# Transposes of the first half of the merged matrix write to PSUM banks of the attention's pool

## The chip, the cores and the metric

The kernel runs on one core of a Trainium2 chip. The metric is the time of one execution on the device in microseconds (us). Several runs of the kernel were timed, and one execution was profiled on the hardware.

## The reference

Two layers of a gated trunk over 256 rows of width 1024, with three branches per layer (an attention in blocks, an attention on selected keys, an attention on a memory), and a final norm. All is fp32. What matters here is the end of each layer: every branch's output (256 x 512) is multiplied by its matrix of w_branch, gated, and the three are summed; the sum goes through w_out.

```python
    ys = jnp.stack([ya, yb, ym], axis=2)
    up = jnp.einsum('bsnw,nwd->bsnd', ys, w_branch)
    gates = jax.nn.sigmoid(mix.reshape(b, s, N_BRANCH, D_MODEL))
    merged = jnp.sum(gates * up, axis=2)
    return x + jnp.einsum('bsd,de->bse', merged, w_out)
```

## The kernel before

**Products.** An fp32 product is made of three fp32r products, `mm3` (lines 105 to 107): high part by high part, high by low and low by high. `split` makes the parts: ACT copies the high part (L101), DVE subtracts it (L102). Weights come in units of 128 x 1024 through `unit`: SP loads `raw` (four buffers), ACT casts it to `whi`, DVE subtracts to `wlo` (four buffers each). So a cast waits until PE has used the unit four before it, and a load until DVE has subtracted the unit four before it.

**PSUM.** There are three pools of banks: pmm with four (tiles mm), psa with two (tiles sc), pst with two (tiles pt). The pools psa and pst serve the attention, the small transposes and, at the layer's end, the accumulators of w_out. A pool gives its banks out in the order in which the program asks for them.

**The end of a layer.** The 256 rows are two tiles t of 128, the 1024 columns of the merged matrix two halves b of 512. `mixes(b, n)` makes the gate by a tanh on ACT (L538). `merge(b, n, ...)` multiplies branch n's output by its weights (24 matmuls, 512 wide), DVE multiplies by the gate (L551) and adds to the sum acc (L553). After the third branch of a half, `merged_T(b, acc)` transposes the sum, per row tile t four 128 x 128 transposes into one bank (L562, a group), ACT writes the high part mgh (L564) and DVE the low part mgl (L565); both are needed by w_out, whose eight units of weights k = 0 to 7 (half 0 for k below 4, half 1 above) accumulate in banks sc and pt per row tile. In layer 0 each row tile has two accumulators of 512; in layer 1 the second tile has 512, 256 and 256 (the last in a bank mm), and behind w_out follow the additions to x (L621), the squares for the norm (L622), the factor rs on POOL (L628), the multiplications by the gain and by rs (L624, L635, L637, L632) and the stores.

**Names used below.** B: the 24 matmuls of `merge(0, 2)`. C: the 24 of `merge(1, 2)`. Both read the branch output in the tile bq. T00, T01: the two groups of transposes of half 0, row tiles 0 and 1; T10, T11: those of half 1. O1 to O8: the eight units of w_out's weights.

**The order.** The program asks for C's banks behind those of `merged_T(0)`: the list `todo` ends with (0, 2) and (1, 2), and `merged_T(b, ...)` follows where n is 2. A scheduler makes each engine's queue from it; it may place later work earlier on an engine, but not past its pool's order of banks. Each engine then works through its queue in order. PE's queue decides how B, the groups, C and w_out follow on each other.

Of the kernel before, what the change touches and what calls it, by code (L numbers as in the profile page):

```python
# [34 lines left out]
def trunk(ctx, tc, x, x_t, mem, mem_t, consts, norm_g, gains, w_grp, w_idx, w_mix, w_kv, w_br, w_o, final_g, out):  # L35
# [6 lines left out]
    pmm = ctx.enter_context(tc.tile_pool(name="pmm", bufs=4, space=PSUM))  # L42
    psa = ctx.enter_context(tc.tile_pool(name="psa", bufs=2, space=PSUM))
    pst = ctx.enter_context(tc.tile_pool(name="pst", bufs=2, space=PSUM))

    def bank(pool, tag):
        return pool.tile([P, 512], F32, tag=tag, name=tag)
# [432 lines left out]
    for l in range(L):  # L480
# [74 lines left out]
        def merged_T(b, acc):  # L555

            bs = slice(4 * b, 4 * b + 4)
            for t in range(NT):
                tt = slice(t * P, (t + 1) * P)
                pt = bank(pmm, "mm")  # L560
                for i in range(4):
                    nc.tensor.transpose(pt[:, i * P:(i + 1) * P], acc[:, t, i * P:(i + 1) * P], ident)  # L562
                pt = pt.rearrange("p (a b) -> p a b", b=P)
                nc.scalar.activation(mh[:, bs, tt], pt, AF.Copy, scale=0.5)  # L564
                nc.vector.scalar_tensor_tensor(ml[:, bs, tt], pt, 0.5, mh[:, bs, tt].bitcast(F32),  # L565
                                               op0=ALU.mult, op1=ALU.subtract)
# [7 lines left out]
        for j, (b, n) in enumerate(todo):  # L574
            if j == 3 and l + 1 < L:
                mhl = mem_tiles()
                memT = big.tile([P, KC, S], F32, tag="big", name="memT")
                load_after(memT, mem_t)
                mem_prep(l + 1, memT, *mhl, range(KC))
            merge(b, n, mxs[j], mxs[2 * b])  # L580
            if j != 2 and len(mxs) < 6:
                mxs.append(mixes(*todo[len(mxs)]))
            if n == 2:
                merged_T(b, mxs[2 * b])
# [26 lines left out]
    for t in range(NT):  # L611
# [4 lines left out]
        for c in cuts[t]:  # L616
            a, b = c
# [90 lines left out]
```

## Time and profile before

| | us |
|---|---|
| median of 3 runs | 632.03 |
| lowest, highest | 631.92, 632.26 |
| the profiled execution, its time | 632.53 |
| the profiled execution, its span | 630.7 |

The span is from the first to the last instruction; the time holds 1.8 us more that lie around it. Sums below are made against the profiled execution, and then moved to the median, which is 0.5 us lower. A row of a timeline gives the start, the duration, the engine, the line of the kernel, the operation, the tile written and the tiles read; in square brackets stands how long the engine was idle before it and what released it. A matmul's duration holds its passage through the array, so successive ones overlap: what it takes of PE's time is the distance of the starts.

### The profile page before, as it was taken

What the parts mean: (1) busy time and instruction counts of PE and PEld (TensorE: products, weight loads), DVE (VectorE), ACT (ScalarE), POOL (GpSimd) and SP (SyncE); (2) the same over time, 40 slices, a digit from 0 to 9 for tenths busy, and PEclk for the clock granted to TensorE, in tenths of its full rate; (3) what the DMA queues carried; (4) which work ended last, traced back from release to release, by engine and by line L of the source; (5) the groups of instructions that cost most, each with busy time, mean ns of one, the idle gap of its engine ahead of it and who ended that gap; (6) DMA issues with size and microseconds to landing.
All of it is one profiled execution on the core that took longest, in us unless ns stands there. A gap on an engine that the chain in (4) does not pass through costs nothing.

```text
span 630.7 us, 10090 instructions
## 1 busy us (share of the span) xinstructions
PE 613.3 (97%) x3518; PEld 536.2 (85%) x3518; DVE 489.7 (78%) x1002; ACT 391.0 (62%) x721; POOL 90.4 (14%) x159
## 2 busy tenths in 40 slices
PE   7999999999999999998999999999999999999894
PEld 5989989888988888887889998998898888888783
DVE  5678889998867878786584778998887787778563
ACT  6758555686657856744464666657675696654342
POOL 1213004003200212110020100310321011221002
PEclk8999999999999999999999999999999999999998
DMA  8966554456554554574655755454555545465521
GB/s 290 347 202 224 173 164 144 134 169 200 160 171 145 180 179 138 197 235 125 194 171 137 265 165 164 140 160 149 181 177 165 165 136 176 160 197 180 155 68 67
DMA packets 31731, 109.57 MB, mean 174 GB/s; under 512 B 3648, under 2 KB 3648, under 8 KB 31552
## 3 DMA queue, kind: packets, MB, share of 16 engines
q1 hardware_dynamic: 31392, 108.39, 53.6%
q8 instruction: 28, 0.46, 0.3%
q10 hardware_dynamic: 288, 0.52, 0.2%
q14 instruction: 23, 0.19, 0.1%
HBM read 107.86 MB, written 1.05 MB: 173 GB/s over the span
## 4 chain that ended last, share of the span: by engine, by line
PE 94%; DVE 2%; ACT 1%; DMA 1%; POOL 1%; issue 1%; SPq 0%; POOLq 0%; DVEq 0%; ACTq 0%
PE mm L107 25%; PE mm L106 25%; PE mm L105 25%; PE sc L107 2%; PE sc L106 2%; PE sc L105 2%; PE sc L297 2%; PE pt L217 1%; PE pt L323 1%; PE pt L107 1%; PE sc L294 1%; PE pt L106 1%; PE pt L105 1%; DMA raw<-in_w_kv 1%; DVE wlo L102 1%
## 5 line engine op out<-in xcount | busy, mean ns | idle before, releaser
L102 DVE TENSOR_TENSOR wlo<-raw,whi 128x1024 fp32r<-128x1024 f32 (+2 forms) x201 | 241.6, 1207 | 73.1 <-ACT whi L101 70.2
L101 ACT CAST whi<-raw 128x1024 fp32r<-128x1024 f32 (+2 forms) x201 | 204.0, 1017 | 122.4 <-PE mm L107 57.6
L107 PE MATMUL mm<-whi,hl 128*128 128x512 f32 (+2 forms) x416 | 160.0, 386 | 1.4 <-DVE hl L102 1.4
L106 PE MATMUL mm<-wlo,hh 128*128 128x512 f32 (+2 forms) x416 | 160.5, 386 | 0.0
L105 PE MATMUL mm<-whi,hh 128*128 128x512 f32 (+2 forms) x416 | 160.1, 387 | 0.0
L107 PEld LDWEIGHTS mm<-whi,hl 128*128 128x128 f32 x416 | 78.1, 188 | 15.8 <-DVE hl L102 1.6
L106 PEld LDWEIGHTS mm<-wlo,hh 128*128 128x128 f32 x416 | 78.3, 188 | 13.8
L105 PEld LDWEIGHTS mm<-whi,hh 128*128 128x128 f32 x416 | 78.1, 188 | 13.3
L284 POOL TENSOR_SCALAR pr<-pr,rinv 128x256 f32<-128x256 f32 (+1 forms) x80 | 44.3, 571 | 221.1 <-DVE rinv L282 219.0
L107 PE MATMUL mm<-hh,wlo 128*128 128x256 f32 x256 | 73.3, 287 | 0.0
L106 PE MATMUL mm<-hl,whi 128*128 128x256 f32 x256 | 72.9, 285 | 0.0
L105 PE MATMUL mm<-hh,whi 128*128 128x256 f32 x256 | 72.4, 283 | 0.0
L106 PEld LDWEIGHTS mm<-hl,whi 128*128 128x128 f32 x256 | 49.0, 191 | 0.2
L105 PEld LDWEIGHTS mm<-hh,whi 128*128 128x128 f32 x256 | 49.0, 191 | 0.2
L107 PEld LDWEIGHTS mm<-hh,wlo 128*128 128x128 f32 x256 | 48.9, 191 | 0.0
L279 ACT ACTIVATE pr<-tm,nb 128x128 f32<-128x128 f32 (+1 forms) x80 | 36.7, 460 | 11.5 <-DVE nb L313 10.7
L206 POOL TENSOR_TENSOR qf<-rt,rt 128x128 f32<-128x128 f32 (+2 forms) x24 | 14.6, 619 | 129.0 <-DVE rt L205 129.0
L553 POOL TENSOR_TENSOR mx<-mx 128x512 f32<-128x512 f32 x8 | 12.4, 1551 | 51.3 <-DVE mx L551 51.3
L551 DVE SCALAR_TENSOR_TENSOR mx<-mx,mm 128x512 f32<-128x512 f32 x24 | 16.4, 684 | 3.5 <-PE mm L107 3.4
L538 ACT ACTIVATE mx<-mm 128x512 f32<-128x512 f32 x24 | 14.3, 596 | 7.7 <-PE mm L107 7.5
L105 PE MATMUL mm<-mh,whi 128*128 128x256 f32 x64 | 18.1, 284 | 0.0
L106 PE MATMUL mm<-ml,whi 128*128 128x256 f32 x64 | 18.1, 283 | 0.0
(259 smaller groups left out, 1140.9 us busy)
## 6 DMA issues: line engine op xcount, KB each, us to landing
raw<-in_w_grp SPq DMA_DIRECT2D x80, 512.0 KB, 4.7
raw<-in_w_mix SPq DMA_DIRECT2D x48, 512.0 KB, 4.0
raw<-in_w_br SPq DMA_DIRECT2D x24, 512.0 KB, 3.8
raw<-in_w_o SPq DMA_DIRECT2D x16, 512.0 KB, 4.5
raw<-in_w_kv SPq DMA_DIRECT2D x15, 512.0 KB, 6.0
raw<-in_w_idx SPq DMA_DIRECT2D x16, 292.0 KB, 3.0
memT<-in_mem_t SPq DMA_DIRECT2D x4, 256.0 KB, 5.8
xr<-in_x SPq DMA_DIRECT2D x2, 512.0 KB, 6.5
```

Source lines behind the costliest of these rows:

```text
L101: nc.scalar.copy(hi, src)
L102: nc.vector.tensor_sub(lo, src, hi.bitcast(F32))
L105: nc.tensor.matmul(o, lh, rh, start=start, stop=False, skip_group_check=True)
L106: nc.tensor.matmul(o, lh, rl, start=False, stop=False, skip_group_check=True)
L107: nc.tensor.matmul(o, ll, rh, start=False, stop=stop, skip_group_check=True)
L206: nc.gpsimd.tensor_tensor(dst[:, :, 0:16], t1[:, :nh], t2[:, :nh], op=ALU.add)
L279: nc.scalar.activation(pr[:, i, :nk], tm[:, i, :nk], AF.Exp, bias=nb[:, i:i + 1], scale=scale, accum_out=rsum[:, i:i + 1])
L284: nc.gpsimd.tensor_scalar(pr[:, i, :nk], pr[:, i, :nk], rinv[:, i:i + 1], 1.0, op0=ALU.mult, op1=ALU.mult)
L297: nc.tensor.matmul(scs[i][:, 1, :], qT[:, h, P:], k[:, b, :], start=b == 0, stop=b == 1, skip_group_check=True)
L538: lambda t, i, ps: nc.scalar.activation(mx[:, t], ps, AF.Tanh, scale=0.5))
L551: nc.vector.scalar_tensor_tensor(mx[:, t], mx[:, t], 1.0, ups[t], op0=ALU.add, op1=ALU.mult)
L553: (nc.gpsimd, nc.vector)[n - 1].tensor_tensor(acc[:, t], acc[:, t], mx[:, t], op=ALU.add)
```

## The change

One line in `merged_T`: for half b = 0 the bank of a group of transposes comes from the pool pst (tile pt); for half 1 it comes from pmm (tile mm) as before.

```diff
             for t in range(NT):
                 tt = slice(t * P, (t + 1) * P)
-                pt = bank(pmm, "mm")
+                pt = bank(*((pst, "pt"), (pmm, "mm"))[b])
                 for i in range(4):
                     nc.tensor.transpose(pt[:, i * P:(i + 1) * P], acc[:, t, i * P:(i + 1) * P], ident)
```

The queues change with it. First PE in layer 0, before, where B ends (mm_3252 is B's second row tile, mm_3293 T00, sc_3363 and pt_3364 w_out's accumulators of row tile 0, whi_3368 O1):

```order
L107 MATMUL mm_3252<-whi_3260,bq_1987 128x512
L562 MATMUL mm_3293<-cst_82,mx_2604 128x128 x4
L105 MATMUL sc_3363<-whi_3368,mgh_2602 128x512
L106 MATMUL sc_3363<-wlo_3369,mgh_2602 128x512
L105 MATMUL pt_3364<-whi_3368,mgh_2602 128x512
L106 MATMUL pt_3364<-wlo_3369,mgh_2602 128x512
L107 MATMUL sc_3363<-whi_3368,mgl_2603 128x512
L107 MATMUL pt_3364<-whi_3368,mgl_2603 128x512
```

And PE in layer 0 now, where T00 stands (mm_3307 and mm_3308 are C's two row tiles):

```order
L107 MATMUL mm_3307<-whi_3316,bq_1987 128x512
L107 MATMUL mm_3308<-whi_3310,bq_1987 128x512
L562 MATMUL pt_3293<-cst_82,mx_2604 128x128 x4
L105 MATMUL mm_3308<-whi_3310,bq_1987 128x512
L106 MATMUL mm_3308<-wlo_3311,bq_1987 128x512
```

A little further down the same queue, where C ends (pt_3300 is T01, mm_3349 T10):

```order
L107 MATMUL mm_3308<-whi_3316,bq_1987 128x512
L562 MATMUL pt_3300<-cst_82,mx_2604 128x128 x4
L105 MATMUL sc_3363<-whi_3368,mgh_2602 128x512
L106 MATMUL sc_3363<-wlo_3369,mgh_2602 128x512
L562 MATMUL mm_3349<-cst_82,mx_2758 128x128 x4
L107 MATMUL sc_3363<-whi_3368,mgl_2603 128x512
L105 MATMUL pt_3364<-whi_3368,mgh_2602 128x512
L106 MATMUL pt_3364<-wlo_3369,mgh_2602 128x512
L107 MATMUL pt_3364<-whi_3368,mgl_2603 128x512
```

Before, w_out followed on T00, and T01 and C stood behind its first twelve products. Now 15 matmuls of C stand ahead of T00, nine between T00 and T01, and w_out begins behind T01; T10 stands behind its second product. Layer 1 has the same pattern. ACT and DVE follow: ACT has the casts of O3 and O4 between the mgh of T00 and that of T01, where they stood behind both; DVE has C's first L551 and L553 ahead of the mgl of T00.

DVE at the kernel's end, before (xr0 and xr1 are the two row tiles, o_6826 the output of the first):

```order
L621 TENSOR_TENSOR xr0_78<-xr0_78,pt_6697 128x512
L624 TENSOR_TENSOR o_6826<-xr0_78,gb_6806 128x512
L621 TENSOR_TENSOR xr1_79<-xr1_79,sc_6698 128x512
L624 TENSOR_TENSOR o_6826<-xr0_78,gb_6806 128x512
L621 TENSOR_TENSOR xr1_79<-xr1_79,pt_6699 128x256
L621 TENSOR_TENSOR xr1_79<-xr1_79,mm_6700 128x256
L635 TENSOR_SCALAR o_6826<-o_6826,rs_6828 128x512
L637 SCALAR_TENSOR_TENSOR o_6857<-xr1_79,rs_6859,gb_6806 128x512
```

And now:

```order
L621 TENSOR_TENSOR xr0_78<-xr0_78,pt_6697 128x512
L624 TENSOR_TENSOR o_6826<-xr0_78,gb_6806 128x512 x2
L621 TENSOR_TENSOR xr1_79<-xr1_79,sc_6698 128x512
L621 TENSOR_TENSOR xr1_79<-xr1_79,pt_6699 128x256
L635 TENSOR_SCALAR o_6826<-o_6826,rs_6828 128x512
L621 TENSOR_TENSOR xr1_79<-xr1_79,mm_6700 128x256
L637 SCALAR_TENSOR_TENSOR o_6857<-xr1_79,rs_6859,gb_6806 128x512
```

L635 has moved ahead of the last addition, and both L624 ahead of the second tile's additions. On PE the last units of w_out finish the first row tile earlier in the queue: 23 matmuls stand behind its last product into sc, where 16 did. On ACT the first tile's L632 stands ahead of the second tile's squares. The queues of SP and POOL are the same as before.

## Rows read from the trace of the kernel before

**Rows 1.** The page, part 1: busy us (share of the span) xinstructions.

```profile
PE 613.3 (97%) x3518; PEld 536.2 (85%) x3518; DVE 489.7 (78%) x1002; ACT 391.0 (62%) x721; POOL 90.4 (14%) x159
```

**Rows 2.** Waits of PE, whole span: engine line waited for: us in total, times, longest.

```profile
PE sc L105 <- ACT mgh L564: 2.4, 2, 1.2
...
PE sc L107 <- DVE mgl L565: 1.1, 2, 0.5
```

**Rows 3.** Timeline of PE, layer 0: start us, us, engine line op, idle before.

```profile
278.98 0.39 PE L105 MATMUL mm<-whi,bq 128*128 128x512 f32 x1
...
284.19 0.40 PE L107 MATMUL mm<-whi,bq 128*128 128x512 f32 x1
284.43 0.60 PE L562 MATMUL mm<-cst,mx 128*128 128x128 f32 x4
286.22 0.50 PE L105 MATMUL sc<-whi,mgh 128*128 128x512 f32 x1 [1.19 <-ACT mgh L564]
...
287.96 0.50 PE L107 MATMUL sc<-whi,mgl 128*128 128x512 f32 x1 [0.54 <-DVE mgl L565]
...
289.91 0.60 PE L562 MATMUL mm<-cst,mx 128*128 128x128 f32 x4
...
290.82 0.40 PE L107 MATMUL mm<-whi,bq 128*128 128x512 f32 x1
...
315.65 0.39 PE L107 MATMUL pt<-whi,mgl 128*128 128x512 f32 x1
```

**Rows 4.** Timeline of PE, layer 1.

```profile
589.54 0.60 PE L562 MATMUL mm<-cst,mx 128*128 128x128 f32 x4
...
595.03 0.60 PE L562 MATMUL mm<-cst,mx 128*128 128x128 f32 x4
...
608.92 0.28 PE L106 MATMUL mm<-wlo,mgh 128*128 128x256 f32 x1
...
610.11 0.28 PE L107 MATMUL mm<-whi,mgl 128*128 128x256 f32 x1
610.58 0.50 PE L105 MATMUL sc<-whi,mgh 128*128 128x512 f32 x1 [0.19 <-ACT whi L101]
...
622.02 0.28 PE L107 MATMUL mm<-whi,mgl 128*128 128x256 f32 x1
```

**Rows 5.** Timeline of ACT, layer 0.

```profile
284.63 1.05 ACT L101 CAST whi<-raw 128x1024 fp32r<-128x1024 f32 x1 [0.31 <-PE mm L107]
285.58 0.59 ACT L564 ACTIVATE mgh<-mm 128x512 fp32r<-128x512 f32 x1
```

**Rows 6.** Timeline of DVE, layer 0.

```profile
280.75 1.23 DVE L102 TENSOR_TENSOR wlo<-raw,whi 128x1024 fp32r<-128x1024 f32 x1 [1.43 <-ACT whi L101]
...
282.62 0.69 DVE L553 TENSOR_TENSOR mx<-mx 128x512 f32<-128x512 f32 x1
...
286.09 1.22 DVE L102 TENSOR_TENSOR wlo<-raw,whi 128x1024 fp32r<-128x1024 f32 x1
287.22 0.68 DVE L565 SCALAR_TENSOR_TENSOR mgl<-mm,mgh 128x512 fp32r<-128x512 f32 x1
```

**Rows 7.** The tile raw, 270 to 320 us: the weight loads.

```profile
DMA to landing us min/median/max: 3.2/4.4/6.4
```

**Rows 8.** Windows, 290 to 300 us: length, busy by engine, PEclk, DMA share, GB/s.

```profile
290.00:300.00 10.00, 10.00 (x50) 8.32 (x49) 6.31 (x8) 5.00 (x6) 0.00 (x0) 1.00 0.24 79
```

**Rows 9.** Timeline of DVE, the end.

```profile
619.79 0.69 DVE L621 TENSOR_TENSOR xr<-xr,sc 128x512 f32<-128x512 f32 x1 [4.59 <-PE sc L107]
...
623.46 1.37 DVE L635 TENSOR_SCALAR o<-o,rs 128x512 f32<-128x512 f32 x1
626.05 0.75 DVE L637 SCALAR_TENSOR_TENSOR o<-xr,rs,gb 128x512 f32<-128x512 f32 x1 [1.23 <-POOL rs L628]
```

**Rows 10.** Timeline of ACT and of POOL, the end.

```profile
624.67 0.18 ACT L622 ACTIVATION_READ_ACCUMULATOR sq<-xr 128x1 f32 x1
...
622.34 0.96 POOL L628 TENSOR_TENSOR rs<-ms,half 128x1 f32<-128x1 f32 x1
```

## The prediction

> **What bounds the kernel now.** I read the page's busy times first, then PE's waits, then PE's timeline at the places those waits point to, then what ACT, DVE and the loads do there. PE is busy for 613.3 of 630.7 us, 97% [rows 1]: only what PE still waits for, and what stands ahead of its first and behind its last matmul, can be won. Of its waits two come twice, once per layer, and belong to the lines of the change: 2.4 us for mgh and 1.1 us for mgl [rows 2]. The timeline shows the place: T00 starts at 284.43, and the next matmul, the first of w_out, only at 286.22, after mgh was written; its third product waits again for mgl and starts at 287.96 [rows 3]. Layer 1 repeats it from 589.54 on [rows 4]. So PE is head-of-line blocked: its queue holds w_out's products right behind the transposes whose eviction they need, while the 24 matmuls C, which need neither, stand behind T01 at 290 us.
>
> **What the change moves.** The program has the same arithmetic and the same instructions; four of the eight transposed banks are called pt and no longer mm. In the pool pmm C's two banks came behind T00's and T01's, so C could not be placed before T01; now they follow mix's and B's directly. In the built order 15 of the 24 C matmuls stand ahead of T00, nine between T00 and T01, and w_out begins behind T01, as the pieces above show. SP's and POOL's order is the same, so the loads are issued in the same order.
>
> **Step 1, the prices on PE.** A 512-wide matmul takes a slot of 0.2265 us: from 278.98 to 284.19 are 23 slots [rows 3]. A 256-wide one takes 0.119: ten slots from 608.92 to 610.11 [rows 4]. Four transposes and the two matmuls behind them take 290.82 - 289.91 = 0.91, so the group costs 0.457 beyond the two [rows 3].
>
> **Step 2, layer 0.** From T00 to the end of w_out PE has 24 C, 96 w_out matmuls and four groups: 120 x 0.2265 + 4 x 0.457 = 29.01 us. It took from 284.43 to 315.65 + 0.23 = 315.88, that is 31.45 [rows 3]. An undisturbed stretch runs a little over these prices: from 595.03 to 610.11 + 0.12 lie 48 wide, 24 narrow and three groups, 15.10 us by the prices, 15.20 in the trace [rows 4], 0.7% more. So 29.2, and **2.25 us** go away if no new wait comes.
>
> **Step 3, layer 1.** Here w_out has 72 wide and 48 narrow products: 96 x 0.2265 + 48 x 0.119 + 1.83 = 29.28, with 0.7% 29.48. It took from 589.54 to 622.02 + 0.12, 32.60 [rows 4]. That is **3.12 us**. More than in layer 0, because PE also waited here for the fifth unit's weights (610.11 to 610.58, and the next wait behind it). ACT casts O5 behind the mgh of T11, and T11 stood only 12 narrow matmuls ahead of O5's first use, 1.9 us with the group; now it stands 26 ahead, six wide and 20 narrow, 4.2 us. The chain needs 0.60 for the transposes, 0.59 for mgh, 1.05 for the cast [rows 3, 5], 2.2 us, and 1.22 more for the subtraction [rows 6], which is wanted five matmuls later.
>
> **Step 4, is there a new wait?** In layer 0's clock: C starts at 284.43. Its weights are there: the second unit's wlo ended at 280.75 + 1.23 = 281.98 [rows 6]. T00 then starts 15 slots on, at 287.83; its acc was ready at 283.31 [rows 6]. C's last starts at 290.10, T01 at 290.33, w_out at 290.79, T10 two slots later, and the first product with mgl at 291.70. Against that:
> - mgh of T00: 287.83 + 0.60 + 0.59 [rows 3, 5] = 289.02, wanted at 290.79.
> - mgl of T00 stands on DVE behind C's first L551 and L553 (C's first half ends at 287.76; two of about 0.7 [rows 6]), so 289.2 + 0.68 = 289.9, wanted at 291.70. Both have 1.8 us to spare.
> - O3 takes the weight buffer that C's first unit leaves at 289.13: cast to 290.2, subtraction to 291.4; wanted at 293.97 and 294.42.
> - O4 follows C's last matmul (290.49): cast to 291.55, then mgh of T01, which is queued behind both casts on ACT, to 292.15. DVE does wlo of O3, an L551, wlo of O4 and then mgl of T01, to 294.0; wanted 24 slots behind 291.70, at 297.1.
> - The pt bank of w_out is T00's own: its first product must wait for T00's eviction, but it needs that mgl anyway. Cost nothing; the cover is the 1.8 us above.
> Every margin is positive, so I take the steps 2 and 3 in full. Behind w_out the order of all queues is the one of before up to the next such place (three matmuls move past a group at the layer's border), so 2.25 us are carried rigidly to layer 1.
>
> **Step 5, the end.** In the new order the first row tile of w_out is finished 23 matmuls before PE's last (eight wide slots, 15 narrow: 3.60 us), so relative to PE's end DVE's first addition can start at 622.02 - 3.60 + 0.39 + 0.04 = 618.85 instead of 619.79 [rows 4, 9], 0.94 earlier. But L635, 1.37 us long, now stands on DVE ahead of the last addition. It waits for POOL's rs, before 622.34 + 0.96 [rows 10], now 622.36, and runs to 623.77; the last addition ends at 624.1 (0.57 later than before) and the last square on ACT at about 624.65, where it was 624.67 + 0.18 = 624.85 [rows 10]. So L637 starts some 0.2 earlier. Bounds: a gain of 0.94 if nothing of L635 is in the way, a loss of 1.37 - 0.94 = 0.43 if all of it is. I take a gain of **0.2**, which the walk gives.
>
> **Sum.** 2.25 + 3.12 + 0.2 = 5.6 us. The profiled execution took 632.53, its changed one 626.9; the median of the runs is 0.5 lower, 632.03, so **626.4 us**. Without the 0.7% and with the best end the gain is 2.44 + 3.32 + 0.94 = 6.7, to 625.3; with twice the 0.7% and the worst end 4.5, to 627.5.
>
> PE's granted clock in the stretch is 1.00 before and behind the waits, 2.4 GHz [rows 8], so the shorter waits win no clock.
>
> **The rivals.**
> - *One layer's wait comes back.* The evictions of T00 run more than 1.8 us late, because DVE and ACT now serve C and T00 in the same 3 us: w_out then waits behind T01 as it waited behind T00. For it: four DVE operations stand ahead of mgl. Against it: DVE is busy for 6.31 of 10 us there [rows 8]. It gives 632.0 - 3.4 = 628.7.
> - *The wait only moves.* PE reaches w_out with C done, so O3 and O4, which use C's buffers, become what it waits for, and the whole 5.4 us come back there. It needs O3's cast 3.8 us late and then 2.25 us more. For it: casts already wait for PE today, 0.31 us at 284.63 [rows 5]. Against it: a cast follows within 0.04 us of the matmul that frees its buffer (284.63 behind 284.19 + 0.40 [rows 3, 5]). It gives 632.0. The Trainium skill has a rule for this outcome: TensorE: Matmul & The Clock Gate, section "HAM oscillation — how this bites in real kernels", reports of one kernel that "Adding PSUM double-buffering gave no further gain". By that rule the time would stay 632.0; here the rows of PE's waits on mgh and mgl [rows 2] speak against it, since PE did wait for a bank's eviction.
> - *Slower: the loads set the pace.* C's 5.4 us of PE work no longer stand between O2 and O3, so O1 to O8 are drawn in one run, a unit of 512 KB every 12 slots, 2.72 us. A load takes 4.4 us to land, at most 6.4 [rows 7]. If two no longer overlap, each unit costs 4.4 - 2.72 = 1.7 us more; the four units O5 to O8, whose loads wait for O1's to O4's subtraction, give 6.7 us per layer: 632.0 - 5.6 + 13.4 = 639.8. It decides from 3.4 us per unit on (5.4 / 2 / 4 = 0.7 above 2.72). Against it: the DMA engines are busy for 0.24 of the time at 290 to 300 us [rows 8], and O2's subtraction, which frees O6's load, ends at 287.31 [rows 6], some 17 us ahead of O6's first use (58 w_out matmuls and two groups behind 290.79, at 304.8).
>
> **Chances.** Forecast 0.83 (625.3 to 627.5), one layer's wait 0.09, the wait moves 0.04, slower 0.04. The range is the forecast's, and goes on to the first rival: 625.2 to 628.8. A measurement of this kernel can tell 0.2% from no change, 1.3 us: faster 0.92, same 0.04, slower 0.04.
>
> **What would show it.** In the changed profile: no wait of PE for mgh or mgl on w_out; T00 about 3.4 us behind B's last matmul; C ahead of w_out without a gap; w_out's last matmul of layer 0 at about 313.4, PE's last at 616.6; no wait for whi of O5 in layer 1; L635 ahead of the last L621. Wrong would be a PE gap behind T01, or one at O3 or O5.

## The result, and the profile after

The changed kernel takes 625.99 us, the median of four runs (625.32 to 626.78), beside 632.08 (631.92 to 632.26) for the kernel before. The ratio is 0.9898, with a 95% interval of 0.9881 to 0.9914: faster by 6.1 us, where 5.6 were forecast. The profiled execution took 626.08 us with a span of 624.3.

First PE's busy time and its waits. The page of the changed kernel, part 1:

```profile
PE 611.6 (98%) x3518; PEld 535.0 (86%) x3518; DVE 489.4 (78%) x1002; ACT 390.2 (63%) x721; POOL 89.2 (14%) x159
```

All waits of PE over the whole span (line, releaser: us in total, times, longest):

```profile
PE pt L73 <- POOL idle L70: 1.5, 1, 1.5
PE mm L105 <- ACT whi L101: 1.4, 2, 1.2
PE mm L105 <- ACT hh L101: 0.7, 1, 0.7
PE mm L106 <- DVE wlo L102: 0.5, 1, 0.5
PE mm L107 <- DVE hl L102: 0.5, 1, 0.5
```

The two lines of [rows 2] are gone. What is left in this execution are waits of the program's first 40 us. The five engines have as many instructions as before [rows 1].

PE's timeline in layer 0 answers to [rows 3]:

```profile
283.84 0.39 PE L105 MATMUL mm<-whi,bq 128*128 128x512 f32 x1
...
287.25 0.60 PE L562 MATMUL pt<-cst,mx 128*128 128x128 f32 x4
...
289.78 0.60 PE L562 MATMUL pt<-cst,mx 128*128 128x128 f32 x4
290.13 0.48 PE L105 MATMUL sc<-whi,mgh 128*128 128x512 f32 x1
...
291.03 0.48 PE L107 MATMUL sc<-whi,mgl 128*128 128x512 f32 x1
...
312.97 0.39 PE L105 MATMUL mm<-whi,mh 128*128 128x512 f32 x1
```

C starts at 283.84 without a gap behind B. T00 starts 3.41 us later, T01 behind the rest of C, and w_out's products of mgh (290.13) and mgl (291.03) start without a bracket, so without a wait. From C's start to the first matmul behind w_out, 312.97, it is 29.13 us, where the same work took 31.45.

The evictions of T00, on ACT and on DVE, end in time:

```profile
287.88 0.60 ACT L564 ACTIVATE mgh<-pt 128x512 fp32r<-128x512 f32 x1 [2.78 <-PE pt L562]
288.59 1.05 ACT L101 CAST whi<-raw 128x1024 fp32r<-128x1024 f32 x1
289.98 1.05 ACT L101 CAST whi<-raw 128x1024 fp32r<-128x1024 f32 x1 [0.34 <-PE mm L107]
```

```profile
288.62 0.68 DVE L565 SCALAR_TENSOR_TENSOR mgl<-pt,mgh 128x512 fp32r<-128x512 f32 x1
```

mgh is there at 288.48 and wanted at 290.13, mgl at 289.30 and wanted at 291.03: 1.65 and 1.73 us to spare. The casts of O3 and O4 follow as soon as C has left the buffers.

At layer 1's end, PE, answering to [rows 4]:

```profile
586.63 0.39 PE L105 MATMUL mm<-whi,bq 128*128 128x512 f32 x1
...
604.88 0.28 PE L107 MATMUL mm<-whi,mgl 128*128 128x256 f32 x1
604.99 0.40 PE L105 MATMUL sc<-whi,mgh 128*128 128x512 f32 x1
...
606.16 0.39 PE L107 MATMUL sc<-whi,mgl 128*128 128x512 f32 x1
...
615.94 0.28 PE L107 MATMUL mm<-whi,mgl 128*128 128x256 f32 x1
```

O5's first product follows 0.11 us behind the last narrow one; before, 0.47 lay between them [rows 4]. From C's start to PE's end there are 615.94 + 0.12 - 586.63 = 29.43 us instead of 32.60. How much of this hung on O5's weights can be read from the same seven products in both traces: the seventh behind that narrow one starts 1.28 us after it (606.16), and in the kernel before, where the narrow one started at 610.11 [rows 4], 2.07 us after it:

```profile
612.18 0.40 PE L107 MATMUL sc<-whi,mgl 128*128 128x512 f32 x1
```

So 0.79 us of layer 1's gain are O5's weights, which come in time now.

The end on DVE, answering to [rows 9], and ACT's last reading of a sum, answering to [rows 10]:

```profile
612.76 0.69 DVE L621 TENSOR_TENSOR xr<-xr,sc 128x512 f32<-128x512 f32 x1 [5.13 <-PE sc L107]
...
616.11 1.48 DVE L635 TENSOR_SCALAR o<-o,rs 128x512 f32<-128x512 f32 x1
617.51 0.41 DVE L621 TENSOR_TENSOR xr<-xr,mm 128x256 f32<-128x256 f32 x1
619.59 0.75 DVE L637 SCALAR_TENSOR_TENSOR o<-xr,rs,gb 128x512 f32<-128x512 f32 x1 [1.67 <-POOL rs L628]
```

```profile
618.28 0.19 ACT L622 ACTIVATION_READ_ACCUMULATOR sq<-xr 128x1 f32 x1
```

L635 stands ahead of the last L621, which starts 1.3 us behind the end of PE's last matmul (615.94 + 0.28). Still, L637 starts 3.65 us behind the start of PE's last matmul, where it was 4.03.

**Where the time went**, each stretch the difference of two starts on the timelines. The columns: the start of B in layer 0; from there to the first matmul behind w_out; from there to B's start in layer 1; from there to the start of PE's last matmul; from there to the last multiplication by rs on DVE (L637 in the kernel before). The rows below the first two are the experiments of the next section.

| kernel | B starts | end of layer 0 | between | end of layer 1 | tail | sum of the four |
|---|---|---|---|---|---|---|
| before | 278.98 | 36.90 | 268.22 | 37.92 | 4.03 | 347.07 |
| the change | 278.40 | 34.57 | 268.22 | 34.75 | 3.65 | 341.19 |
| the change, again | 278.89 | 34.57 | 268.22 | 34.75 | 3.66 | 341.20 |
| layer 0 alone | 278.48 | 34.56 | 268.22 | 37.94 | 4.02 | 344.74 |
| layer 1 alone | 278.12 | 36.89 | 269.69 | 34.75 | 3.67 | 345.00 |
| T00 alone in pst | 278.38 | 36.90 | 268.22 | 37.89 | 4.02 | 347.03 |
| T01 alone in pst | 278.41 | 34.58 | 268.22 | 34.78 | 3.42 | 341.00 |
| all in pmm, issued later | 278.37 | 35.09 | 268.22 | 35.41 | 3.43 | 342.15 |
| both halves in pst | 279.38 | 34.56 | 268.22 | 35.54 | 4.03 | 342.35 |
| the change with another tail | 277.88 | 34.57 | 268.22 | 34.75 | 2.89 | 340.43 |

The change gains 2.33 us at the end of layer 0, 3.17 at the end of layer 1 and 0.38 in the tail, 5.88 in all; between the two layers not a hundredth is lost. The spans differ by 6.4, because B also started 0.58 us earlier. That is not the change's: with the queues of the kernel before (T00 alone in pst) B starts at 278.38.

### The profile page after: what moved, and what is told of

Its sections match the earlier page's. It is cut to its first block, busy times and chain, and to the rows that moved or that the text cites. A ratio compares the mean times of both kernels' runs of the same rounds, so it can differ in the third digit from the quotient of the medians.

```text
span 624.3 us, 10089 instructions
## 1 busy us (share of the span) xinstructions
PE 611.6 (98%) x3518; PEld 535.0 (86%) x3518; DVE 489.4 (78%) x1002; ACT 390.2 (63%) x721; POOL 89.2 (14%) x159
## 3 DMA queue, kind: packets, MB, share of 16 engines
HBM read 107.86 MB, written 1.05 MB: 174 GB/s over the span
## 4 chain that ended last, share of the span: by engine, by line
PE 93%; DMA 3%; DVE 1%; ACT 1%; SPq 0%; issue 0%; POOL 0%; POOLq 0%; ACTq 0%
PE mm L107 25%; PE mm L105 24%; PE mm L106 24%; PE sc L107 2%; PE sc L105 2%; PE sc L106 2%; PE sc L297 2%; PE pt L217 1%; DMA xT<-in_x_t 1%; PE pt L323 1%; DMA raw<-in_w_kv 1%; PE pt L105 1%; DMA xr<-in_x 1%; PE pt L106 1%; PE pt L107 1%; PE sc L294 1%
## 5 line engine op out<-in xcount | busy, mean ns | idle before, releaser
L284 POOL TENSOR_SCALAR pr<-pr,rinv 128x256 f32<-128x256 f32 (+1 forms) x80 | 43.0, 555 | 221.6 <-DVE rinv L282 219.5
L553 POOL TENSOR_TENSOR mx<-mx 128x512 f32<-128x512 f32 x8 | 12.4, 1551 | 51.9 <-DVE mx L551 51.9
L107 PE MATMUL mm<-mh,wlo 128*128 128x256 f32 x64 | 18.0, 284 | 0.0
```

The lines of the kernel that those rows point to most:

```text
L107: nc.tensor.matmul(o, ll, rh, start=False, stop=stop, skip_group_check=True)
L284: nc.gpsimd.tensor_scalar(pr[:, i, :nk], pr[:, i, :nk], rinv[:, i:i + 1], 1.0, op0=ALU.mult, op1=ALU.mult)
L553: (nc.gpsimd, nc.vector)[n - 1].tensor_tensor(acc[:, t], acc[:, t], mx[:, t], op=ALU.add)
```

## The experiments

The theory: what pays is the order on PE. T01's banks stood ahead of C's in the pool pmm, so C stood behind T01, and nothing without a wait was left between T00 and w_out. The rivals: a free bank pays by itself; the two layers' gains are not independent; pst is the better pool for all transposes.

**T00 alone in pst.**

```diff
-                pt = bank(pmm, "mm")
+                pt = bank(*((pst, "pt"), (pmm, "mm"))[b or t])
```

> Only T00's two banks come from pst; T01 stays in pmm as before. In the built program the order of the instructions on every engine is that of the kernel before, only the bank's name differs. Theory (the order on TensorE, T00 behind C, is what pays; the bank by itself pays nothing): 632.0 us, and in layer 0 and layer 1 the matmuls of w_out wait for mgh and mgl as before (some 1.2 and 0.5 us in layer 0). Rival (a free bank in pst pays by itself, through evictions of pmm that come earlier): a good part of the gain, some 629 us, with the two waits shorter.

Measured: 632.66 us (631.25 to 633.87, ten runs) beside 632.29 for the kernel before on the same chip, ratio 0.9994 (0.9978 to 1.0011). Its timeline of PE in layer 0:

```profile
283.82 0.60 PE L562 MATMUL pt<-cst,mx 128*128 128x128 f32 x4
285.62 0.50 PE L105 MATMUL sc<-whi,mgh 128*128 128x512 f32 x1 [1.20 <-ACT mgh L564]
...
287.36 0.50 PE L107 MATMUL sc<-whi,mgl 128*128 128x512 f32 x1 [0.54 <-DVE mgl L565]
```

T00 writes to a bank of pst (pt), and every wait is still there. The bank of T00 by itself pays nothing.

**T01 alone in pst.**

```diff
-                pt = bank(pmm, "mm")
+                pt = bank(*((pst, "pt"), (pmm, "mm"))[b or 1 - t])
```

> Only T01's two banks come from pst; T00 stays in pmm. In the built order T00 then stands right behind B, all 24 matmuls of C follow, then products of w_out from the sc banks for O1 and O2, T01, and the rest. Theory (what pays is that work without a wait stands between T00 and the first product of mgh and mgl): the whole gain, 626.0 us, no wait for mgh or mgl in w_out although T00's bank is one of pmm. Rival (T00 itself must lie outside pmm): 629 us or more, with waits for mgh or mgl left, or with C waiting for T00's pmm bank.

Measured: 626.62 us (625.89 to 627.09) beside 632.29, ratio 0.9899 (0.9869 to 0.9929), the whole gain. PE in layer 0:

```profile
283.86 0.60 PE L562 MATMUL mm<-cst,mx 128*128 128x128 f32 x4
284.21 0.49 PE L105 MATMUL mm<-whi,bq 128*128 128x512 f32 x1
...
289.79 0.39 PE L105 MATMUL sc<-whi,mgh 128*128 128x512 f32 x1
...
291.16 0.60 PE L562 MATMUL pt<-cst,mx 128*128 128x128 f32 x4
```

T00 stays in pmm (mm) right behind B, C follows it, and T01 comes six products into w_out. In the table the gain is 6.07 us. So it is T01's bank that held C back. These two runs together separate the order from the bank.

**All in pmm, issued later.** The transposes of both halves are written behind the last merge.

```diff
-            if n == 2:
-                merged_T(b, mxs[2 * b])
+            if j == 5:
+                for half_b in range(2):
+                    merged_T(half_b, mxs[2 * half_b])
```

> All transposes keep their pmm banks; instead the transposes of both halves are issued in the program only behind the last merge, so that on TensorE B and C stand ahead of T00, T01 and T10. Theory (order alone): B to T00 without an idle stretch, but T00's own eviction, casts and subtraction are then covered by T01, T10 and nothing of C; with T10 there too, some 1.8 us of work against the 1.8 to 2.5 us that the chain from T00 to mgl takes, so most of the gain, 626 to 628 us. Rival (the banks of pst are needed, since pmm's have to be emptied first): 632 us, with the same idle time in front of other instructions.

Measured: 627.32 us (627.02 to 627.34) beside 632.29, ratio 0.9907 (0.9882 to 0.9931). No bank comes from pst, and 4.92 of the 5.88 us are there. PE in layer 0:

```profile
289.25 1.47 PE L562 MATMUL mm<-cst,mx 128*128 128x128 f32 x12
291.05 0.50 PE L105 MATMUL sc<-whi,mgh 128*128 128x512 f32 x1 [0.32 <-ACT mgh L564]
291.39 0.39 PE L106 MATMUL sc<-wlo,mgh 128*128 128x512 f32 x1
```

Three groups almost cover the chain behind T00: 1.80 us lie between T00's start and the first product, 0.32 of it idle. The two layers' ends are 0.52 and 0.66 us longer than with the change. In layer 0 this place holds all of it: by the prediction's prices three groups and a product take 3 x 0.457 + 0.2265 = 1.60 us, and here the second product starts 2.14 us behind T00. Layer 1 shows the same idle bracket; the 0.14 more there is not located.

**Layer 0 alone, layer 1 alone.**

```diff
-                pt = bank(pmm, "mm")
+                pt = bank(*((pst, "pt"), (pmm, "mm"))[b or l])
```

> The change in layer 0 alone; layer 1 as before. Theory (the two layers' gains are separate and carried on unchanged): 2.3 us less than before, 629.7 us, from the end of B in layer 0; layer 1 keeps its waits for mgh, mgl and for O5's whi. Rival (what one layer gains the next gives back to the loads or to a fixed point): 632.0 us, with an additional wait for a load between the layers.

```diff
-                pt = bank(pmm, "mm")
+                pt = bank(*((pst, "pt"), (pmm, "mm"))[b or 1 - l])
```

> The change in layer 1 alone; layer 0 as before. Theory: layer 1's 3.2 us and the tail's 0.2 to 0.4 us, so 3.4 us less than before, 628.6 us; layer 0 keeps its waits for mgh and mgl. With the run of layer 0 alone the two gains add up to that of the change. Rival (the gains overlap): the two single gains add up to more than that of the change by a microsecond or more.

Measured: layer 0 alone 629.35 us (628.65 to 630.58) beside 632.29, ratio 0.9946 (0.9927 to 0.9966); layer 1 alone 628.70 (628.39 to 629.62) beside 632.55, ratio 0.9939 (0.9921 to 0.9958). In the table the first gains 2.34 at the end of layer 0 and nothing else, the second 3.17 + 0.36 at the end of layer 1 and in the tail. The sum is 5.87, the change's 5.88: the gains are independent. This rests on the stretches, for the medians can't tell it: they give 2.94 and 3.85, together 6.79, where the change gave 6.23 on the second chip, and each of the two intervals is 1.2 us wide to either side. In the run of layer 0 alone, layer 1 (PE's waits, 575 to 626 us) still has all three:

```profile
PE sc L105 <- ACT mgh L564: 1.2, 1, 1.2
PE sc L107 <- DVE mgl L565: 0.5, 1, 0.5
PE sc L105 <- ACT whi L101: 0.2, 1, 0.2
```

The profiled execution of layer 1 alone was 1.47 us longer between the layers. In a stretch there that the change doesn't touch, a load of weights came late, and PE waited for POOL. ACT's timeline, PE's waits between 313 and 585 us, and POOL's timeline:

```profile
353.52 1.05 ACT L101 CAST whi<-raw 128x1024 fp32r<-128x1024 f32 x1 [3.30 <-DMA raw<-in_w_grp]
```

```profile
PE pt L217 <- POOL qf L206: 1.0, 2, 0.7
```

```profile
356.27 1.58 POOL L206 TENSOR_TENSOR qf<-rt,rt 128x80 f32<-128x80 f32 x2 [35.39 <-DVE rt L205]
```

In the kernel before, the longest wait of ACT for a load between 345 and 362 us is 1.3, PE waits for nothing in that stretch, and the same two operations of POOL take 0.60 us (at 354.43). PE did not wait for the late load itself; that the load led to POOL's slower qf is likely from the order in time, but not shown. That execution took 629.62 us, the other three 628.39 to 628.78, so I count it as chance.

**Both halves in pst.**

```diff
-                pt = bank(pmm, "mm")
+                pt = bank(pst, "pt")
```

> The transposes of both halves take pst's banks. w_out's pt accumulators must then wait until T10 and T11 are evicted, and the products of the sc accumulators move ahead. Theory (order pays, and pst's banks are free only until w_out's pt accumulators want them): 626 us if the sc products cover T10's and T11's eviction; each uncovered eviction would show as a wait of a pt matmul for ACT or DVE, up to 2 us in a layer, so 626 to 630 us. Rival (pst is as good for half 1 as for half 0 and frees pmm further): below 625 us.

Measured: 627.74 us (627.14 to 628.24) beside 632.55, ratio 0.9921 (0.9904 to 0.9939); the change itself, on the same chip, 626.32. The time is in the expected range, but not for the expected reason. No pt product waits for an eviction. Layer 0 keeps its gain; layer 1 loses 0.79 us, and the tail loses its gain of 0.38: DVE's first addition starts 2.23 us ahead of PE's last matmul again, as in the kernel before [rows 4, 9]. Weight loads into PE that wait, 590 to 618 us, and PE around them:

```profile
PEld sc L105 <- ACT whi L101: 0.3, 1, 0.3
PEld sc L106 <- DVE wlo L102: 0.3, 1, 0.3
```

```profile
605.91 0.28 PE L107 MATMUL pt<-whi,mgl 128*128 128x256 f32 x1
...
607.85 0.39 PE L107 MATMUL sc<-whi,mgl 128*128 128x512 f32 x1
```

And ACT from 596 to 612 us, first here, then in the change:

```profile
601.90 0.60 ACT L564 ACTIVATE mgh<-pt 128x512 fp32r<-128x512 f32 x1 [6.13 <-PE pt L562]
605.15 3.90 ACT L101 CAST whi<-raw 128x1024 fp32r<-128x1024 f32 x4 [2.65 <-PE pt L107]
```

```profile
601.42 0.60 ACT L564 ACTIVATE mgh<-mm 128x512 fp32r<-128x512 f32 x1 [6.63 <-PE mm L562]
601.92 2.94 ACT L101 CAST whi<-raw 128x1024 fp32r<-128x1024 f32 x3
```

With T10 and T11 in pst, w_out's pt accumulators stand behind them in the pool, so PE does the other products of O1 to O4 first and keeps all four weight buffers until 605 us. Counted from B's start in layer 1 (582.16 here, 581.19 in the change), O5's cast starts 22.99 us behind it instead of 20.73. From the narrow product ahead of O5 to the seventh behind it PE takes 1.94 us (605.91 to 607.85) where the change takes 1.28, so O5's weights are 0.66 of the 0.79; the other 0.13 is not located.

**The change with another tail, and the change again.** In the first, row tile 0's scaling stands behind row tile 1's last square and last addition.

```diff
-            nc.vector.tensor_add(xr[t][:, a:b], xr[t][:, a:b], oacc[t][c][:, :b - a])
-            nc.scalar.activation(sq[:, a:b], xr[t][:, a:b], AF.Square, scale=1.0 / 32, accum_out=ms[-1])
+            added = nc.vector.tensor_add(xr[t][:, a:b], xr[t][:, a:b], oacc[t][c][:, :b - a])
+            squared = nc.scalar.activation(sq[:, a:b], xr[t][:, a:b], AF.Square, scale=1.0 / 32, accum_out=ms[-1])
...
-        nc.scalar.activation(o[:, :512], o[:, :512], AF.Copy, scale=rs)
+        with tc.issue_after(squared.ins):
+            nc.scalar.activation(o[:, :512], o[:, :512], AF.Copy, scale=rs)
...
-            nc.vector.tensor_scalar(o[:, 512:], o[:, 512:], rs, None, op0=ALU.mult)
+            with tc.issue_after(added.ins):
+                nc.vector.tensor_scalar(o[:, 512:], o[:, 512:], rs, None, op0=ALU.mult)
```

> The change, and in the tail the scaling of row tile 0 (L632 and L635) put behind the last square and the last addition of row tile 1. Theory (in the tail of the changed kernel row tile 0's L635, 1.48 us on VectorE, stands ahead of the last L621 that the end hangs on): the last L621 starts at PE's end instead of 1.3 us behind it, the end comes some 1.0 us earlier, 625.0 us. Rival (row tile 0's own scaling and its store then end last): 626 us or more, with L635 or the store of row tile 0 at the end of the chain.

> The changed kernel as it is, on the same chip as the others for comparison: 626.0 us.

Measured: 625.43 us (624.78 to 625.87), ratio 0.9885 (0.9867 to 0.9902), and 626.32 (626.08 to 626.57), ratio 0.9898 (0.9878 to 0.9918), both beside 632.55. The ranges of the two don't meet, and the table's tails differ by 0.77: it is faster than both kernels. DVE's end in it (its lines 637 and 639 are 635 and 637 of the others), and POOL's:

```profile
615.74 0.42 DVE L621 TENSOR_TENSOR xr<-xr,mm 128x256 f32<-128x256 f32 x1
616.08 1.00 DVE L637 TENSOR_SCALAR o<-o,rs 128x512 f32<-128x512 f32 x1
618.31 0.75 DVE L639 SCALAR_TENSOR_TENSOR o<-xr,rs,gb 128x512 f32<-128x512 f32 x1 [1.23 <-POOL rs L628]
```

```profile
615.53 1.27 POOL L624 TENSOR_TENSOR o<-xr,gb 128x512 f32<-128x512 f32 x1
616.78 0.85 POOL L626 TENSOR_SCALAR ms<-ms 128x1 f32<-128x1 f32 x2
```

The last addition starts 0.32 us behind the start of PE's last matmul (615.42), where it was 1.57, so 1.25 earlier; of this 0.77 reach the end, not the 1.0 expected. Some 0.18 is lost ahead of the end of the last square on ACT, which comes 1.46 us behind the start of PE's last matmul (616.70 + 0.18 here) where it was 2.53, and 0.31 behind it: 1.43 us lie from there to the last multiplication, where it was 1.12. Both additions of POOL (L626) now follow on its L624, where one of them had been done while the last square was still to come.

## Why the prediction was right, step by step

The forecast was 626.4 us with a range of 625.2 to 628.8. The measured median lies 0.4 below the forecast, inside the range and inside the likeliest case's own bounds (625.3 to 627.5).

- **The reading.** PE was blocked by the order of its queue. The two runs with one of T00 and T01 in pst show it: the same bank changed for T00 gains nothing, for T01 all. The prediction named both groups' banks as what held C back; it was T01's. One thing more stood in the rows and went unused: ACT cast O2 until 284.63 + 1.05 = 285.68 ahead of mgh, though T00's transposes ended at 284.43 + 0.60 = 285.03, and DVE subtracted O2 until 287.31 ahead of mgl, though mgh was there at 286.17 [rows 3, 5, 6]. Another order on these two engines might have shortened the waits as well; no run tried it.
- **Steps 1 and 2, layer 0:** 29.2 us priced, 29.13 measured; 2.25 forecast, 2.33 gained. The stretch ran 0.4% above the bare prices, not 0.7%.
- **Carried to layer 1:** rigid, as assumed; the stretch between is 268.22 in both.
- **Step 3, layer 1:** 29.48 priced, 29.43 measured; 3.12 forecast, 3.17 gained, with no wait at O5, whose share is 0.79.
- **Step 4, the margins:** 1.8 us each forecast, 1.65 and 1.73 measured. O3's and O4's casts came where the step put them, against C's start within 0.1 us.
- **Step 5, the tail:** 0.2 forecast, 0.38 measured. The step had the first addition right (3.17 us ahead of the start of PE's last matmul, measured 3.18) and L635 ahead of the last one. It took POOL's rs of the first row tile 0.2 us too late. From this come 0.1: L635 started 0.2 earlier than the step had it and ran 0.11 longer (1.48 for 1.37). The other 0.08 came behind the last square: 1.12 us to L637 where it was 1.20.
- **The sum:** 5.6 forecast, 5.88 measured from B's start; each of the three terms came out a little above its forecast, the tail by most (0.18). The 6.1 between the medians holds 0.2 more, which no run assigns; B's start alone differs by 1.5 between executions.
- **The rivals.** No wait came back, none moved to O3 or O4, and no load set the pace: in the profiled execution PE waited for nothing behind the first 40 us. Against the first rival the prediction held that DVE is busy for 6.31 of 10 us, but that row is of 290 to 300 us [rows 8]. Where T00's evictions run, DVE is nearly full in the changed kernel, 5.59 of 6 us (the row has PE, PEld, DVE, ACT and POOL in this order), so the margins of 1.65 and 1.73 us were there although DVE had little time free. The granted clock is 1.00 there too.

```profile
284.00:290.00 6.00, 6.00 (x32) 4.91 (x31) 5.59 (x8) 2.73 (x4) 0.00 (x0) 1.00 0.72 240
```

  The sentence of the Trainium skill that stood beside the second rival (TensorE: Matmul & The Clock Gate, section "HAM oscillation — how this bites in real kernels") reports no further gain from PSUM double-buffering; taken as a rule for other banks, it would have given nothing here. The trace disagrees, by 5.88 us: the section is about a kernel whose TensorE waited for DMA, and here PE waited for an eviction. The run with T00 alone in pst, 0.9994, is the case in this kernel that behaves as the sentence says.

## What to carry to other kernels

When the queue of the busiest engine waits for an eviction, look which work without a wait stands behind, and what keeps it there: here it was a later group's place in a pool's order, one bank request away from the group that waits. Price such a change by the distances of the starts at that one place, not by the idle brackets: the two brackets of layer 0 add up to 1.73 us [rows 3], and 2.33 were gained. A bracket begins only where the duration of the instruction before it ends (T00: 284.43 + 0.60), later than its slot, and the first product behind a wait takes more than a slot (0.34 us from 291.05 to 291.39 with all in pmm, against 0.2265). Then check each eviction and each buffer against its new time of need; 1.7 us to spare were enough for a rigid gain. A pool that is free now may be wanted by the next stage: giving it half 1 too cost 1.2 us, 0.66 of it through weight buffers held longer.

## What the runs showed of the hardware that was not expected

- The program's start differs between executions by more than some of the effects above: B started between 277.88 and 279.38 us in ten profiles. Two of the three latest starts (the kernel before, 278.98, and both halves in pst, 279.38) had a mean granted clock of 0.91 of full speed over the first 20 us, the eight others 1.00. The row of the kernel before, then of the change (us, busy by engine, PEclk, DMA share, GB/s):

```profile
0.00:20.00 20.00, 16.58 (x58) 11.41 (x59) 10.66 (x15) 12.91 (x20) 2.58 (x14) 0.91 0.84 300
```

```profile
0.00:20.00 20.00, 16.59 (x61) 10.49 (x62) 10.82 (x15) 13.04 (x20) 2.14 (x12) 1.00 0.84 291
```

  The third, the change again (278.89), had 1.00, so the clock alone doesn't sort them. What the three have in common is PE's wait for POOL's qf at 51 to 52 us: 0.44, 0.62 and 0.78 us, where the seven others have 0.20 or none. Whether one of these causes the other is not shown. The row of the change again:

```profile
51.45 0.33 PE L217 MATMUL pt<-cst,qf 128*128 128x128 f32 x1 [0.78 <-POOL qf L206]
```

- Behind the start the chip repeats itself to a few hundredths: the stretch between the layers took 268.22 us in nine of ten profiles. The tenth took 1.47 more; it had the one late load, for which ACT waited 3.30 us, and PE's two waits for POOL, 1.0 us.
